# A two-layer GELU network by Winograd-Strassen products: sums written over dead blocks, w2 blocks brought in one go, the first layer's sums stored one superblock later

## The chip, the cores and the metric

One core of a Trainium2 chip runs the kernel. The metric is the device time of one execution in microseconds (us), given as the median over several executions. Its engines have their own instruction streams, each in order: TensorE (PE in the profile, with its weight loads as PEld), VectorE (DVE), ScalarE (ACT), GpSimd (POOL) and SyncE (SP). In this kernel SP and POOL issue the DMA transfers (SPq and POOLq in the profile).

## The reference

```python
def reference(x, w1, w2):          # x 8x1024x1024, w1 1024x4096, w2 4096x1024, fp32
    h = x @ w1
    h = 0.5 * h * (1 + np.tanh(np.sqrt(2 / np.pi) * (h + 0.044715 * h ** 3)))
    return (h @ w2).astype(np.float32)
```

The first two axes of x are one axis of 8192 tokens.

## The kernel before

**Strassen products.** Tokens are taken in 8 superblocks of 1024 (loop L639). In each, both matrix products are done in fp16 by seven products of half-size blocks instead of eight (tables A_TERMS for the operand from x or g, B_TERMS for that from w1 or w2, L28 to L45). Each operand is cut into 2x2 blocks named 11, 12, 21, 22. Five of the seven weight operands are a sum or difference of two blocks ("sums"; products 4, 1, 3, 7, 6), two are plain blocks (2 and 5). Likewise five x operands are differences. The weight sums are needed by every superblock, so they are made once, stored in DRAM (w1_d, w2_d) and loaded in later superblocks; the plain fp16 blocks are kept in raw_d and raw2_d.

**Memory.** Pool `up` has 26 units of 512 KB (128 partitions x 2048 fp16), shared by weight blocks, sums and x operands (all called u in the profile). Pool `tp` has 10 tiles tmp (128x512 fp32), `gcp` 4 tiles gc. There are 8 PSUM banks ps. A tile is handed out again when its last reader is done, and for a tile that is being stored this means when the DMA has landed.

**matmul1** (L277). For each of 16 chunks c of 128 columns: seven products of four matmuls (L283), in the order 4, 5, then 6 of the chunk before (`finish`, L297), 1, 2, 3, 7. Three banks take them; DVE forms the results with the `tt` helper (all its operations are recorded at L112), through tmp tiles, and ACT copies a bank (L347) and applies GELU into g (L293). Four chunks share a quad of w1 columns. In superblocks 0 and 1 a quad is a MadeQuad (L150): raw blocks, from which DVE makes five sums of 128x2048. In superblock 0 the raw blocks are loaded from w1 in fp32 and cast; in superblock 1 they come from raw_d (L160), and each sum is stored to w1_d by a POOL DMA (L192). From superblock 2 on, `load_ops` (L198) loads all seven operands of a quad. `ahead` (L305) brings the next quad step by step during the current one.

**matmul2_made** (L381) does the second product in superblocks 0 and 1: products 4, 2, 5, 1, 7, 3, 6 in this order, each of four row groups q of 16 matmuls (`product2`, L561). Where the g operand is a difference, DVE makes it into a gc tile ahead of the row group. `bring` loads w2 blocks (superblock 0: fp32 with a cast on POOL, L123; superblock 1: fp16 from raw2_d), `keep` stores the plain blocks to raw2_d, `add` makes the sums of w2, and in superblock 1 stores them to w2_d (L421). Blocks 11 and 21 come first, already during matmul1; 22 and 12 follow. Banks are evicted by ACT copies (L437, L428) and DVE additions; u and d are intermediate results that later products are added to. Outputs are stored from tmp tiles on the POOL queue (L379), at most eight POOL DMAs outstanding. In superblock 1, `split_inner` (L474) forms the parts of the sums 7 and 6 for a second level of Strassen and stores them to in_d. From superblock 2 on, `matmul2` (L599) loads w2_d and in_d and doesn't differ between the two kernels.

**x of the next superblock.** `x_cast` (L256) has POOL issue 8 DMAs that cast x to fp16 in DRAM (xb); `x_transpose` (L263) has SP issue 16 transposing DMAs into four units. Before matmul1, `XOps.make` forms five differences of x blocks on DVE.

**Order.** A list scheduler orders each engine's instructions by data and program order. `load_in_order` (L119) fixes the order of the SP DMAs that use it. `tc.issue_after` ties an instruction behind another. Each engine and each queue runs in the order so found: an instruction that waits holds all behind it on its engine.

Of the kernel before, what the change touches and what calls it, by code (L numbers as in the profile page):

```python
# [56 lines left out]
def kernel(  # L57
# [71 lines left out]
    def make_sum(ops, m, raw, rows, cols, sl=slice(None)):  # L129
# [7 lines left out]
        tt(ops[m][:, :, sl], raw[u][:, :, sl], raw[v][:, :, sl], op)  # L137

    def cast_in(dst, src, cast, staged=False):
# [10 lines left out]
    class MadeQuad:  # L150


        def __init__(self, q, first):
            self.q, self.first, self.ops = q, first, {}
            self.raw = raw_units(KH, QW)
            for m in PLAIN:
                self.ops[m] = self.raw[B_TERMS[m][0]]
            if not first:
                for b, t in self.raw.items():
                    nc.sync.dma_start(out=flat(t), in_=raw_d[q][:, BLOCKS.index(b), :])  # L160
# [28 lines left out]
        def sum(self, m, sl=slice(None)):  # L189
            make_sum(self.ops, m, self.raw, KH, QW, sl)  # L190
            if not self.first:
                nc.gpsimd.dma_start(out=w1_d[self.q][:, m - 1, :], in_=flat(self.ops[m]))  # L192
# [84 lines left out]
    def matmul1(xs, sb):  # L277
# [14 lines left out]
        def gelu(b, c, src):  # L292
            nc.scalar.activation(out=g[b][:, c, :], in_=src, func=GELU)  # L293

# [10 lines left out]
        def ahead(q, step):  # L305

            if q == NI // QC:
                return
            if sb > 1:
                if step == 0:  # L310
                    quads.append(load_ops(w1_d[q], raw_d[q], ORDER, KH, QW))
                return
            if step == 0:
                quad = MadeQuad(q, sb == 0)
                quads.append(quad)
# [6 lines left out]
        if sb == 0:  # L322
            quads.append(MadeQuad(0, True))
            xs.make(5)
# [14 lines left out]
        for c in range(NI):  # L339
            q, j = divmod(c, QC)  # L340
            if j == 0:
                ahead(q + 1, 0)
            w = (quads[q] if sb > 1 else quads[q].ops, slice(j * P, (j + 1) * P))
            pb, qb = psum(), psum()
# [36 lines left out]
    def matmul2_made(sb, g, keep_w1):  # L381
# [3 lines left out]
        sums = {}  # L385
        blocks = None

        def bring(bs, staged):
            for q in range(NI // QC):
                for b in bs:  # L390
                    t = unit(QC, OH)
                    raw[b].append(t)
                    if sb:
                        nc.sync.dma_start(out=flat(t), in_=raw2_d[q][:, BLOCKS.index(b), :])
                        continue
                    for j in range(0, QC, 2):
# [3 lines left out]
                            w2v[int(b[1]) - 1, int(b[0]) - 1, :, c:c + 2, :],  # L400
                            pool_copy,
                            staged,
# [9 lines left out]

        def add(m):
            u, op, v = B_TERMS[m]
            sums[m] = []
            for q in range(NI // QC):
                t = unit(QC, OH)
                tt(t, raw[u][q], raw[v][q], op)
# [11 lines left out]

        v, c21 = {}, {}
        pb, qb, rb = [], [], []
        bring(("11", "21"), False)
        add(4)
        for q, ps in product2(g, 4, pieces(4), pb, True, True):
            v[q] = temp()
            nc.scalar.copy(out=v[q], in_=ps)  # L437
        bring(("22",), True)
        if sb == 0:
            xb = x_cast(1, pool_last[0])  # L440
        keep(("11", "21"))
        for q, ps in product2(g, 2, pieces(2), pb, False):
            _, c21[q] = copy_out("21", q, ps)
        add(1)
        u, d = halves()[1], halves()[1]
        for q, ps in product2(g, 5, pieces(5), qb, True):
            tt(u[q], v[q], ps, SUB)
            tt(d[q], u[q], c21[q], SUB)
        add(7)
        bring(("12",), True)  # L450
        for q, ps in product2(g, 1, pieces(1), rb, True):
            tt(d[q], d[q], ps, ADD)
        if sb == 0:
# [228 lines left out]
```

## Time and profile before

| | us |
|---|---|
| median of 6 runs (1583.75 to 1588.0) | 1585.97 |
| the profiled execution | 1583.75 |
| its span in the trace | 1582.0 |
| PE busy in the span | 1549.0 (98%) |
| DVE busy | 1011.6 (64%) |
| ACT busy | 457.7 (29%) |
| POOL busy | 224.8 (14%) |

The median of the runs is 2.2 us above the profiled execution, and that execution 1.75 above its span. Mean DMA traffic is 227 GB/s over the span. The largest groups that the change touches:

```profile
## 5 line engine op out<-in xcount | busy, mean ns | idle before, releaser
...
L293 ACT ACTIVATE g<-tmp 128x512 f16<-128x512 f32 x256 | 161.1, 630 | 297.5 <-DVE tmp L112 297.4
...
L112 DVE TENSOR_TENSOR u<-u 128x2048 f16<-128x2048 f16 (+2 forms) x150 | 163.7, 1127 | 17.8 <-DMA u<-raw_d 9.0
...
L112 DVE TENSOR_TENSOR gc<-g,g 128x2048 f16<-128x2048 f16 x112 | 137.1, 1257 | 20.1 <-PE ps L566 20.1
```

A row reads: line, engine, operation, what it writes and reads with partitions x elements and type, and the count; then its busy time in us and the mean of one in ns; then the engine's idle time just before such instructions, and what ended most of it. So 20.1 us of DVE idle time before the g differences were ended by a matmul that had read the gc tile.

DMA rows give the transfers, their size and the median time from issue to landing:

```profile
u<-raw_d SPq DMA_DIRECT2D x128, 512.0 KB, 8.2
w_d<-u POOLq DMA_DIRECT2D x40, 512.0 KB, 7.1
out_dram<-tmp POOLq DMA_DIRECT2D x72, 256.0 KB, 3.1
raw_d<-u SPq DMA_DIRECT2D x32, 512.0 KB, 7.9
xb<-in_x_dram POOLq DMA_DIRECT2D x56, 256.0 KB, 11.4
```

### The profile page before, as it was taken

To read this page: it belongs to the slowest core of one execution; us is meant where nothing else is said; L and a number is where in the kernel's file an instruction comes from. 1 tells how busy PE (TensorE), PEld (TensorE's weight loads), DVE (VectorE), ACT (ScalarE), POOL (GpSimd) and SP (SyncE) were. 2 spreads that over 40 slices of the span, in tenths; PEclk is the share of its full clock that TensorE was granted. 3 is DMA by queue.
4 is the path that set the end of the run, shared out by engine and by line. 5 is a ranking of instruction groups with operands and counts; after the bars stand their busy time and mean duration, and the time that the engine had idled before them with its cause. 6 is when DMAs were issued, how large, how long until landed. Compare 5 with 4: busy or idle time off the path is not lost.

```text
span 1582.0 us, 20386 instructions
## 1 busy us (share of the span) xinstructions
PE 1549.0 (98%) x7808; PEld 766.6 (48%) x7808; DVE 1011.6 (64%) x1263; ACT 457.7 (29%) x776; POOL 224.8 (14%) x306
## 2 busy tenths in 40 slices
PE   7999989999989999999999999999999999999998
PEld 4444434444434455444554445544555445544455
DVE  7877767668755566555675557656475565755564
ACT  5641014420144211441124410344103430044200
POOL 2244321012400013000120001200012001200000
PEclk9999999999999999999999999999999999999999
DMA  9988698645984567735686346954469545663155
GB/s 318 340 322 282 173 381 279 192 180 210 387 286 133 187 239 262 253 97 200 253 283 224 119 173 253 330 182 176 151 240 363 150 171 189 239 271 133 54 213 187
DMA packets 167362, 358.93 MB, mean 227 GB/s; under 512 B 72928, under 2 KB 79072, under 8 KB 166368
## 3 DMA queue, kind: packets, MB, share of 16 engines
q1 hardware_dynamic: 148672, 285.26, 51.2%
q0 software_dynamic: 18592, 72.37, 13.9%
q8 instruction: 61, 1.00, 0.2%
q14 instruction: 37, 0.30, 0.1%
HBM read 278.92 MB, written 93.32 MB: 235 GB/s over the span
## 4 chain that ended last, share of the span: by engine, by line
PE 85%; DMA 7%; DVE 4%; issue 2%; POOL 0%; ACT 0%; SPq 0%; DVEq 0%; ACTq 0%; POOLq 0%
PE ps L283 45%; PE ps L566 35%; PE ps L522 6%; DVE u L112 3%; DMA u<-w_d 2%; DMA out_dram<-tmp 2%; DVE tmp L112 1%; DMA u<-raw_d 1%; DMA in_d<-u 1%; DMA gc<-in_w_dram 1%; DMA u<-in_d 0%; DVE gc L112 0%; DMA u<-in_x_dram 0%; POOL in_d L487 0%; ACT g L293 0%
## 5 line engine op out<-in xcount | busy, mean ns | idle before, releaser
L283 PE MATMUL ps<-u 128*128 128x512 f16 x3584 | 784.2, 381 | 19.4 <-DVE tmp L112 14.7
L112 DVE TENSOR_TENSOR tmp<-tmp,ps 128x512 f32<-128x512 f32 x548 | 375.2, 686 | 306.1 <-ACT tmp L347 119.3
L283 PEld LDWEIGHTS <-u 128*128 128x128 f16 x3584 | 351.5, 98 | 449.7 <-issue 27.8
L566 PE MATMUL ps<-u,gc 128*128 128x512 f16 x1792 | 389.4, 379 | 0.0
L566 PEld LDWEIGHTS <-gc 128*128 128x128 f16 x1792 | 175.2, 98 | 211.6
L293 ACT ACTIVATE g<-tmp 128x512 f16<-128x512 f32 x256 | 161.1, 630 | 297.5 <-DVE tmp L112 297.4
L566 PE MATMUL ps<-u,g 128*128 128x512 f16 x1024 | 224.3, 379 | 0.4 <-DVE u L112 0.2
L293 ACT ACTIVATE g<-ps 128x512 f16<-128x512 f32 x256 | 151.9, 596 | 101.8 <-PE ps L283 101.6
L112 DVE TENSOR_TENSOR u<-u 128x2048 f16<-128x2048 f16 (+2 forms) x150 | 163.7, 1127 | 17.8 <-DMA u<-raw_d 9.0
L566 PEld LDWEIGHTS <-g 128*128 128x128 f16 x1024 | 100.2, 98 | 120.6 <-issue 1.8
L112 DVE TENSOR_TENSOR gc<-g,g 128x2048 f16<-128x2048 f16 x112 | 137.1, 1257 | 20.1 <-PE ps L566 20.1
L379 POOL DMA_DIRECT2D out_dram<-tmp x72 | 39.5, 548 | 774.6 <-ACT tmp L616 632.3
L112 DVE TENSOR_TENSOR u<-u,ps 128x512 f32<-128x512 f32 x152 | 101.2, 682 | 71.6 <-ACT tmp L623 37.3
L522 PE MATMUL ps<-u,gc 128*128 128x256 f16 x960 | 109.7, 273 | 0.8
L347 ACT COPY tmp<-ps 128x512 f32<-128x512 f32 x128 | 72.9, 570 | 94.1 <-PE ps L283 94.1
L522 PEld LDWEIGHTS <-gc 128*128 128x128 f16 x960 | 93.8, 98 | 12.8 <-issue 1.6
L112 DVE TENSOR_TENSOR gc<-u 128x2048 f16<-128x2048 f16 x60 | 73.2, 1221 | 38.9 <-PE ps L566 38.9
L112 DVE TENSOR_TENSOR tmp<-ps,tmp 128x512 f32<-128x512 f32 x128 | 88.4, 690 | 10.0 <-DMA out_dram<-tmp 4.1
L112 DVE TENSOR_TENSOR u<-tmp,ps 128x512 f32<-128x512 f32 x32 | 22.0, 687 | 83.7 <-PE ps L566 74.0
L112 DVE TENSOR_TENSOR u<-g,g 128x2048 f16<-128x2048 f16 x48 | 59.6, 1280 | 0.0
L616 ACT COPY tmp<-ps 128x512 f32<-128x512 f32 x24 | 14.1, 586 | 152.0 <-PE ps L566 152.0
L545 POOL TENSOR_TENSOR u<-u,tmp 128x512 f32<-128x512 f32 x12 | 26.2, 2180 | 198.8 <-DMA u<-in_d 140.0
(33 smaller groups left out, 354.6 us busy)
## 6 DMA issues: line engine op xcount, KB each, us to landing
u<-w_d SPq DMA_DIRECT2D x192, 512.0 KB, 8.4
u<-raw_d SPq DMA_DIRECT2D x128, 512.0 KB, 8.2
u<-in_d SPq DMA_DIRECT2D x84, 512.0 KB, 7.4
gc<-in_w_dram SPq DMA_DIRECT2D x48, 512.0 KB, 5.8
w_d<-u POOLq DMA_DIRECT2D x40, 512.0 KB, 7.1
out_dram<-tmp POOLq DMA_DIRECT2D x72, 256.0 KB, 3.1
raw_d<-u SPq DMA_DIRECT2D x32, 512.0 KB, 7.9
xb<-in_x_dram POOLq DMA_DIRECT2D x56, 256.0 KB, 11.4
```

The costliest lines, as they stand in the source:

```text
L112: nc.vector.tensor_tensor(out=out, in0=in0, in1=in1, op=op)
L283: nc.tensor.matmul(bank, lhsT=ops[m][:, k, cs], rhs=xs[m][:, k, :], start=(first and k == 0), stop=(k == KH - 1), skip_group_check=not first,)
L293: nc.scalar.activation(out=g[b][:, c, :], in_=src, func=GELU)
L347: nc.scalar.copy(out=v, in_=pb)
L379: return queue.dma_start(out=out2[r0:r0 + P, o0:o0 + OH], in_=src)
L522: nc.tensor.matmul(bank[:, i * HO:(i + 1) * HO], lhsT=t[:, c, i * P:(i + 1) * P], rhs=y[j][:, c, :], start=(first and i == 0 and c == 0), ...
L545: nc.gpsimd.tensor_tensor(out=part("11"), in0=part("11"), in1=pair(u), op=ADD)
L566: nc.tensor.matmul(banks[q], lhsT=a, rhs=pieces[c // QC][:, c % QC, :], start=(first and c == 0), stop=(c == NI - 1), skip_group_check=not ...
L616: nc.scalar.copy(out=c21, in_=ps)
```

## The change

Six edits, all in superblocks 0 to 2; the matmuls and their order stay as they are.

1. Sums 7, 3 and 6 of w2 are written in place over the raw blocks 21, 22 and 11 (`over=`), which no later product reads.
2. u and d lie in tmp tiles: u is a DVE copy of product 4's bank (before, an ACT copy v, then a separate u), d overwrites the copy-out tile of block 21, and the results of products 7 and 6 are added in place and stored from there.
3. Blocks 22 and 12 are both brought right after product 4, and ScalarE casts them instead of POOL, after the last GELU of matmul1 (`late_copy`). All four raw blocks are kept at once after that.
4. x of the next superblock is cast after the second store of block 21, and transposed ahead of product 1, in both superblocks 0 and 1 (before: superblock 1's followed matmul1's program text, with the cast behind the last store of the superblock before).
5. The raw2_d loads and the transposes of superblock 1 go in program order on SP, and `split_inner` comes ahead of products 7 and 3 instead of behind products 7 and 6.
6. The w1 sums are stored in superblock 2 instead of 1. Superblock 2 therefore makes its quads from raw blocks (16 loads, 20 sums on DVE, 20 stores) instead of loading 28 operands; superblocks 3 to 7 load them as before.

```diff
-        def __init__(self, q, first):
-            self.q, self.first, self.ops = q, first, {}
+        def __init__(self, q, first, store):
+            self.q, self.store, self.ops = q, store, {}
...
         def sum(self, m, sl=slice(None)):
             make_sum(self.ops, m, self.raw, KH, QW, sl)
-            if not self.first:
+            if self.store:
                 nc.gpsimd.dma_start(out=w1_d[self.q][:, m - 1, :], in_=flat(self.ops[m]))
...
-            if sb > 1:
+            if sb > 2:
...
-                quad = MadeQuad(q, sb == 0)
+                quad = MadeQuad(q, sb == 0, sb == 2)
...
+        def late_copy(out, in_):
+            with tc.issue_after(gelu_last[0].ins):
+                nc.scalar.copy(out=out, in_=in_)
...
                     if sb:
-                        nc.sync.dma_start(out=flat(t), in_=raw2_d[q][:, BLOCKS.index(b), :])
+                        load_in_order(flat(t), raw2_d[q][:, BLOCKS.index(b), :])
...
-        def add(m):
+        def add(m, over=None):
...
-                t = unit(QC, OH)
+                t = unit(QC, OH) if over is None else raw[over][q]
...
-        v, c21 = {}, {}
+        u, d = {}, {}
         pb, qb, rb = [], [], []
-        bring(("11", "21"), False)
+        bring(("11", "21"), pool_copy, False)
         add(4)
         for q, ps in product2(g, 4, pieces(4), pb, True, True):
-            v[q] = temp()
-            nc.scalar.copy(out=v[q], in_=ps)
-        bring(("22",), True)
-        if sb == 0:
-            xb = x_cast(1, pool_last[0])
-        keep(("11", "21"))
+            u[q] = temp()
+            nc.vector.tensor_copy(out=u[q], in_=ps)
+        bring(("22",), late_copy, True)
+        bring(("12",), late_copy, True)
+        keep(("21", "22", "11", "12"))
         for q, ps in product2(g, 2, pieces(2), pb, False):
-            _, c21[q] = copy_out("21", q, ps)
+            at, d[q] = copy_out("21", q, ps)
+            if q == 1:
+                xb = x_cast(sb + 1, at)
         add(1)
-        u, d = halves()[1], halves()[1]
         for q, ps in product2(g, 5, pieces(5), qb, True):
-            tt(u[q], v[q], ps, SUB)
-            tt(d[q], u[q], c21[q], SUB)
-        add(7)
-        bring(("12",), True)
+            tt(u[q], u[q], ps, SUB)
+            tt(d[q], u[q], d[q], SUB)
+        add(7, over="21")
+        blocks = x_transpose(xb, load_in_order)
         for q, ps in product2(g, 1, pieces(1), rb, True):
             tt(d[q], d[q], ps, ADD)
-        if sb == 0:
-            blocks = x_transpose(xb, load_in_order)
-        keep(("22", "12"))
-        for q, ps in product2(g, 7, pieces(7), rb, False):
-            c = temp()
-            tt(c, u[q], ps, ADD)
-            store(sb, "11", q, c)
         if sb:
             split_inner(7, pieces(7))
-        add(3)
-        add(6)
+        for q, ps in product2(g, 7, pieces(7), rb, False):
+            tt(u[q], u[q], ps, ADD)
+            store(sb, "11", q, u[q])
+        add(3, over="22")
+        add(6, over="11")
+        if sb:
+            split_inner(6, pieces(6))
         for q, ps in product2(g, 3, pieces(3), qb, False):
             copy_out("12", q, ps)
         for q, ps in product2(g, 6, pieces(6), qb, False):
-            c = temp()
-            tt(c, d[q], ps, ADD)
-            last = store(sb, "22", q, c)
-        if sb:
-            split_inner(6, pieces(6))
+            tt(d[q], d[q], ps, ADD)
+            last = store(sb, "22", q, d[q])
         return last, blocks
...
-        if sb and sb + 1 < NSB:
-            blocks = x_transpose(x_cast(sb + 1, last), nc.sync.dma_start)
-        if sb == 0:
-            last, blocks = matmul2_made(sb, g, quad.keep_raw)
-        elif sb == 1:
-            last, _ = matmul2_made(sb, g, None)
+        if sb < 2:
+            last, blocks = matmul2_made(sb, g, None if sb else quad.keep_raw)
         else:
+            if sb + 1 < NSB:
+                blocks = x_transpose(x_cast(sb + 1, last), nc.sync.dma_start)
             last = matmul2(sb, g)
```

More of the change, by code (lines that the diff above doesn't have):

```diff
@@ L137, in make_sum @@
         tt(ops[m][:, :, sl], raw[u][:, :, sl], raw[v][:, :, sl], op)
+    gelu_last = [None]
     def cast_in(dst, src, cast, staged=False):
@@ L292, in gelu @@
         def gelu(b, c, src):
-            nc.scalar.activation(out=g[b][:, c, :], in_=src, func=GELU)
+            gelu_last[0] = nc.scalar.activation(out=g[b][:, c, :], in_=src, func=GELU)
         late = None
@@ L322, in matmul1 @@
         if sb == 0:
-            quads.append(MadeQuad(0, True))
+            quads.append(MadeQuad(0, True, False))
             xs.make(5)
@@ L342, in matmul1 @@
                 ahead(q + 1, 0)
-            w = (quads[q] if sb > 1 else quads[q].ops, slice(j * P, (j + 1) * P))
+            w = (quads[q] if sb > 2 else quads[q].ops, slice(j * P, (j + 1) * P))
             pb, qb = psum(), psum()
@@ L385, in matmul2_made, with bring @@
         sums = {}
-        blocks = None
-        def bring(bs, staged):
+        def late_copy(out, in_):
+            with tc.issue_after(gelu_last[0].ins):
+                nc.scalar.copy(out=out, in_=in_)
+        def bring(bs, cast, staged):
             for q in range(NI // QC):
@@ L400, in bring @@
                             w2v[int(b[1]) - 1, int(b[0]) - 1, :, c:c + 2, :],
-                            pool_copy,
+                            cast,
                             staged,
```

## The prediction

> **What bounds the kernel now.** I read four views: the engine totals of the page, the busy table cut at the stage ends, the waits of TensorE (PE), and the timeline around the places the first three point to. The totals show an almost full PE:
>
> ```profile
> PE 1549.0 (98%) x7808; PEld 766.6 (48%) x7808; DVE 1011.6 (64%) x1263; ACT 457.7 (29%) x776; POOL 224.8 (14%) x306
> ```
>
> The change leaves the matmuls and their order alone, so only idle PE and PE at a low clock can be won. The stage table says where these are: matmul1 and matmul2 of superblock 0, of superblock 1, then matmul1 of superblock 2, then of 3.
>
> ```profile
> core 0: us, PE busy (x) PEld busy (x) DVE busy (x) ACT busy (x) POOL busy (x), PEclk, DMA share, GB/s
> 17.30:121.10 103.80, 100.10 (x449) 44.01 (x450) 85.39 (x114) 58.47 (x94) 38.18 (x36) 0.98 0.94 327
> 121.10:218.30 97.20, 97.01 (x449) 43.63 (x446) 67.26 (x62) 8.26 (x14) 34.33 (x36) 1.00 0.82 252
> 218.30:326.20 107.90, 100.58 (x450) 44.45 (x450) 78.59 (x105) 44.83 (x78) 17.87 (x34) 0.97 0.74 253
> 326.20:423.50 97.30, 97.08 (x450) 43.84 (x448) 73.20 (x83) 8.27 (x14) 27.00 (x48) 1.00 0.68 258
> 423.50:528.40 104.90, 98.99 (x450) 44.31 (x449) 55.07 (x80) 45.53 (x79) 6.09 (x12) 0.97 0.65 218
> ...
> 622.20:718.90 96.70, 96.70 (x450) 43.83 (x448) 55.00 (x80) 45.74 (x79) 5.48 (x11) 1.00 0.62 202
> ```
>
> Each stage has 448 matmuls, and the undisturbed one takes 96.7 us (0.216 each). Against that, matmul1 of superblock 1 loses 11.2 and of superblock 2 loses 8.2; the two matmul2 between lose 0.5 and 0.6. So 20.5 us is the ceiling. The first stage (7.1 lost) isn't touched. The waits name VectorE (DVE):
>
> ```profile
> PE ps L283 <- DVE tmp L112: 14.7, 11, 5.9
> PE ps L283 <- DVE u L112: 4.3, 3, 2.5
> ```
>
> The timeline of the first gap gives the chain backwards:
>
> ```profile
> 176.44 21.26 SPq L120 DMA_TRANSPOSE u<-xb  x16
> 197.75 8.38 SPq L120 DMA_DIRECT2D raw_d<-u  x8
> 206.23 47.88 SPq L160 DMA_DIRECT2D u<-raw_d  x16
> 217.40 1.23 DVE L112 TENSOR_TENSOR u<-u 128x2048 f16<-128x2048 f16 x1 [8.72 <-DMA u<-raw_d]
> 220.04 0.68 DVE L112 TENSOR_TENSOR tmp<-u,ps 128x512 f32<-128x512 f32 x1
> 227.11 9.72 PE L283 MATMUL ps<-u 128*128 128x512 f16 x32 [4.80 <-DVE tmp L112]
> ...
> 439.84 5.50 PE L283 MATMUL ps<-u 128*128 128x512 f16 x15 [5.91 <-DVE tmp L112]
> ```
>
> SyncE (SP) issues late loads, then 21 us of transposes, then 8 stores of raw w2, and only at 206 the w1 loads for the next superblock. They land at 217. DVE sits 8.7 us on them, with the evictions of product 6 queued behind: their out stores go late, the 10 tmp tiles run short, and PE idles 4.80 and some small pieces, 7.3 in all. The clock then stands at half until 232.4, which makes up nearly all of the other 3.9. The second gap (5.91, and half clock to 444, 2.3) has the other root of this kind: stores of inner sums (in_d) and w2 sums fill the queue from 403 on, and an out store issued at 425.40 takes 13.57 us in the chain of waits, which keeps a tmp tile.
>
> **The change, part by part.** *In-place sums.* Sums 7, 3, 6 overwrite raw blocks 21, 22, 11; u and d stay in tmp tiles. 12 units of sums and 4 of u, d fall away out of 26. No DVE sum is removed. What it buys is time of loading: the last 8 w2 pieces, spread over 141–176 before, find buffers as soon as product 4 has read its operands (134.9). 16 keeps at 1.05 each (8 in 8.38 above) and the 16 transposes (21.3) follow; transposes end near 177 instead of 198, quad 0's w1 loads are issued right behind and, at the 10 us of the row 208.87 (u<-raw_d in the chain), land near 187. DVE needs them from about 191: five x sums and five w1 sums at 1.2 make 11, done near 202, and product 6's first eviction is due at 207.7. Slack some 5 us. So the 8.72 goes, and the evictions of product 6 leave on time.
>
> What is late next: w1 quad 2 takes units that product 6 reads to the last group (216.3); at 10.6 us (median of u<-raw_d at 200–260) they land at 227, and DVE meets the first of their sums after some six chunk evictions, a wait of a few us with evictions behind it. Chunk 1 has 4 free tmp tiles by then, so I take 1.2 lost (0 to 4) for matmul1 of superblock 1, against 11.2.
>
> *Copies.* u is a DVE copy of a bank, not an ACT copy: 4 per superblock by 0.69 (the row of a 128x512 bank operation), 5.5 for both. DVE is 69% busy there (67.26 of 97.20), PE waits for none: 0. Without cover 2.8 each.
>
> *ScalarE casts.* 16 casts at 1041 ns (row L145) are 16.6 us on ACT, which is 8% busy in that stage, in place of 24.6 on POOL (row L123, 1558 each). Product 5 needs block 22 at 148.7; the eighth cast can end near 144 (loads land in 5.5). Hidden, 5 us of cover. The last casts end near 155, ahead of their keeps.
>
> *A new wait.* Here is a cost. In the new DVE order, d += product 1 of row groups 0 and 1 stand ahead of the difference of g that product 1's row group 2 multiplies. The second d waits for row group 1's last matmul, so PE idles through 0.69 + 1.22 and two hand-overs, about 2.3 us. Whether the clock falls is the question, and trace rows on both sides are near:
>
> ```profile
> 17.30 1.78 PE L283 MATMUL ps<-u 128*128 128x512 f16 x4 [2.45 <-DVE u L112]
> 18.00:19.00 1.00, 1.00 (x3) 0.15 (x1) 0.38 (x1) 0.00 (x0) 1.00 (x2) 0.50 1.21 292
> 24.36 5.91 PE L283 MATMUL ps<-u 128*128 128x512 f16 x26 [1.46 <-DVE u L112]
> ```
>
> After 2.45 idle, PE ran at half clock (0.50) from 17.5 to 20.6, a loss of 1.6; after 1.46 it kept full clock. 2.3 is nearer to 2.45: I take 2.3 + 1.5 = 3.8 (2.0 to 3.9), so matmul2 of superblock 0 becomes 101.0.
>
> The Trainium skill, page "TensorE: Matmul & The Clock Gate", Part 1, says the clock falls after at least one idle window of about 3.4 us; by that rule 2.3 us would cost no clock, and the total would be 1.5 lower. The startup row contradicts it, and the measurement goes into the sum.
>
> *Moved x work.* The 8 xb casts of a superblock go behind the second 21 store. Stores 3 and 4 of block 21 queue behind them on POOL, and the d differences of groups 2 and 3, which overwrite the stored tiles, wait for their landings. Before, at the same place, the casts were issued at 144.3 to 147.7 and landed in 4.1 (median), and the two stores behind them, issued at 148.70 and 149.95, took 9.7 and 9.0: landed at 159. Those two d (0.6 each), four in-place sums (1.16 each in a row of four, 4.6) and the first d += (0.7) stand ahead of the second d +=, which can start at 169.4: they must start by 169.4 - 0.7 - 4.6 - 1.2 = 162.9. Covered by 4 us. For superblock 2, xb and transposes leave matmul1 of superblock 1 (226–298) for the middle of its matmul2: DMA moves, no PE work.
>
> *Superblock 1, matmul2.* in_d and w2 sums leave earlier (split 7 ahead of product 7, split 6 ahead of product 3), so fewer stand ahead of the out stores at 403–430. Some DVE sums now wait for in_d landings (8.3 to 9.7 us) with evictions behind: I take 0.3 (0 to 2) on 97.3: 97.6.
>
> *w1 sums.* 20 stores of 0.5 MB (10.5 MB) leave superblock 1, and superblock 2 makes the sums itself: 20 at 1.27 = 25.4 more on DVE (55.1 to 80.5 of 97, fits), 12 loads fewer, 20 stores more. In its first 23 us, 10 sum stores, 4 quad loads and out stores are 5.2 + 2.1 + 2.1 = 9.4 MB, 410 GB/s. The row of 200–260 shows what this traffic does: 402 to 415 GB/s at a share of 1.0, with out stores landing in 9. Quad 2's loads then come about 3 us late. I take 3.5 lost (0.5 to the full 8.2) against 8.2.
>
> **Sum.** Four stages after: 101.0 + 97.9 + 97.6 + 100.2 = 396.7. Before: 97.2 + 107.9 + 97.3 + 104.9 = 407.3. Saved 10.6. The profiled execution took 1583.75 (span 1582.0 and 1.75 around it), so 1573.15; the median of the runs is 2.2 above that execution, so as a median 1575.4.
>
> **Rivals.** *The second gap stays* (0.22). For it: 9.4 MB in 23 us is saturation, the very state in which the first gap stood. Superblock 2 keeps its 8.2, the saving falls by 4.7: 1580.1. Against it: no in_d stores pile up there any more.
>
> *It does not bring the loads forward* (0.08). The transposes wait for xb, which waits for a full queue, or the late loads wait longer for their buffers, so quad 0 is late by more than its 5 us. At 8 to 10 late, superblock 1 keeps 8 to 10 of its 11.2 us; superblock 2 wins 4.7, and 4.1 are lost in the two matmul2: 1.8 to 3.8 saved, 1582.2 to 1584.2, counted as no change.
>
> *Slower: a d that waits for its store* (0.10). The wait just named, of d of group 3 for the 21 store behind the xb casts. With the longest rows (xb 13.8, then an out store's 13.57, from 143.4) the landing is at 170.7, 7.8 late: PE idles 7.8 + 2.3, and the half clock costs 2.3 more (as after 5.91), 12.4 in all. Against it stand the 10.0 won in superblock 1 less 0.3; where superblock 2 keeps its 8.2 nothing else does, and the time is 1588.7. Break-even is a landing at 168, and from 171.2 on it is slower by over 0.2%; 3 us beyond the longest rows, 1592. Against it: the rows of the same place land at 159. For it: 16 keeps of 0.5 MB (8.4 MB) now run in these microseconds, where before the DMA share fell to 0.46 by 160–170.
>
> **Numbers.** Forecast 0.60, second gap 0.22, not forward 0.08, slower mechanism 0.10. 0.2% is 3.2 us, about what a measurement of this kernel can tell from no change. Faster by more than that: all of the forecast and second-gap cases, 0.82. Same: the third case and 0.02 of the last, 0.10. Slower: 0.08. Range: below, 1.2 + 0.3 + 3.5 + 1.8 of my losses not occurring give 1568.6, so 1568; above, the second gap kept and the upper bounds in superblock 1's two stages (2.8 + 1.7) give 1584.6, so 1584.
>
> **What would show it.** Right: no wait of DVE for raw_d loads ahead of product 6's evictions, transposes of superblock 1 ending near 177, stages of 101.0, 97.9, 97.6, 100.2, one PE wait of about 2.3 on DVE's gc in product 1 followed by a clock of 0.50. Wrong: an out store's landing over 9 us ahead of matmul1 of superblock 2 with idle PE (second gap), xb issued after 150 (third), a DVE wait on an out store or raw2 keep before 175 (fourth).

## The result and the profile after

| | us |
|---|---|
| before, median of 38 runs (1583.75 to 1589.46) | 1586.85 |
| changed kernel, median of 17 runs (1579.76 to 1591.78) | 1582.93 |
| ratio, 95% interval | 0.998 (0.9972 to 0.9988) |
| profiled execution of the changed kernel (span 1576.7) | 1578.52 |

The change saves 3.9 us, 0.2%. Measured twice more, with 7 and 5 runs of it, it saved 6.9 and 5.3 us (ratios 0.9961 and 0.9963). The forecast was 10.6. So the sign was right and the size was not, and the runs spread over 12 us where those of before spread over 6.

The busy table of the changed kernel, cut at its stage ends (same order and columns as before):

```profile
122.50:223.60 101.10, 98.50 (x449) 44.10 (x448) 75.19 (x77) 21.14 (x26) 12.21 (x23) 0.98 0.87 274
223.60:321.20 97.60, 97.23 (x450) 43.84 (x449) 69.32 (x95) 45.05 (x78) 3.08 (x6) 1.00 0.36 126
321.20:418.30 97.10, 96.82 (x449) 43.82 (x448) 82.90 (x94) 5.91 (x10) 34.88 (x64) 1.00 1.01 334
418.30:519.80 101.50, 98.59 (x449) 44.17 (x448) 66.24 (x92) 45.23 (x78) 11.85 (x23) 0.98 0.64 209
```

The forecast for these four was 101.0, 97.9, 97.6 and 100.2. In this execution they sum to 397.3 against 396.7. That closeness is luck: two more traces, below, give 399.9 and 401.1. Of the 11.2 us that superblock 1's matmul1 lost, all but 0.9 are gone, as forecast. At the eviction of product 6, where VectorE came late before because it sat 8.72 us on a load, it now waits for TensorE:

```profile
213.46 0.69 DVE L112 TENSOR_TENSOR tmp<-tmp,ps 128x512 f32<-128x512 f32 x1 [4.16 <-PE ps L567]
```

TensorE's waits have changed places:

```profile
PE ps L285 <- ACT tmp L349: 3.9, 3, 2.9
PE ps L567 <- DVE gc L112: 2.6, 1, 2.6
```

The wait on gc is the new one in product 1; the 2.9 on ACT's tmp is the start of superblock 2, at 430.02. There VectorE sits on a w1 load, with evictions behind it:

```profile
419.03 7.28 DMA u<-raw_d
426.41 1.23 DVE L112 TENSOR_TENSOR u<-u 128x2048 f16<-128x2048 f16 x1 [4.29 <-DMA u<-raw_d]
430.02 10.34 PE L285 MATMUL ps<-u 128*128 128x512 f16 x40 [2.90 <-ACT tmp L349]
```

The first row is from the chain that ended last; in it, the load leaves right behind a sum of VectorE that ended at 419.02. The timeline shows the wait in product 1, and the queue of SP around it, with the clock just behind:

```profile
137.41 29.14 SPq L120 DMA_DIRECT2D raw_d<-u  x16
167.49 25.21 SPq L120 DMA_TRANSPOSE u<-xb  x16
192.82 57.79 SPq L162 DMA_DIRECT2D u<-raw_d  x16
166.56 4.63 DVE L112 TENSOR_TENSOR u<-u 128x2048 f16<-128x2048 f16 x4
171.10 1.28 DVE L112 TENSOR_TENSOR tmp<-tmp,ps 128x512 f32<-128x512 f32 x2
172.29 4.63 DVE L112 TENSOR_TENSOR gc<-g,g 128x2048 f16<-128x2048 f16 x4
173.57 22.58 PE L567 MATMUL ps<-u,gc 128*128 128x512 f16 x96 [2.60 <-DVE gc L112]
174.00:175.00 1.00, 1.00 (x4) 0.29 (x2) 1.00 (x2) 0.00 (x0) 0.00 (x0) 0.50 2.17 311
```

The in-place sum 7 (166.56, four pieces), both additions to d (171.10), and only then the g difference that row group 2 needs (172.29): PE idles 2.60 us and then runs at half clock (0.50 in each of the three us from 174 to 177).

But this execution took 1578.52 and the median run 1582.93. A trace of one execution could not say where the other runs lose their time, and the four stages are not the whole: this execution is 5.2 us under the profiled one of before, while the stages alone are 10.0 better. Of the 4.8 between, 1.4 lie ahead of these stages (the first matmul1 takes 102.8 to 106.1 us over the traces of all kernels), 0.4 behind the fourth stage, and 3.0 at the end of the span, where nothing computes:

```profile
1568.00:1573.00 5.00, 1.07 (x10) 0.70 (x8) 0.80 (x2) 0.00 (x0) 0.00 (x0) 1.00 0.57 211
1573.00:1576.70 3.70, 0.00 (x0) 0.00 (x0) 0.00 (x0) 0.00 (x0) 0.00 (x0) 0.53 0.00 0
```

The same two rows of before:

```profile
1576.00:1581.00 5.00, 1.30 (x12) 0.92 (x10) 1.04 (x2) 0.00 (x0) 0.00 (x0) 0.98 0.56 210
1581.00:1582.00 1.00, 0.00 (x0) 0.00 (x0) 0.00 (x0) 0.00 (x0) 0.00 (x0) 0.50 0.00 0
```

In both kernels the last stores end some 3 us after the last matmul (DMA 0.57 and 0.56 of 5 us). Then the changed kernel's span goes on for at least 3.7 us with no engine and no DMA at work, that of before for 1 to 2.

### The profile page after: what moved, and what is told of

Same layout as the page of the kernel before. It is cut to its first block, busy times and chain, and to the rows that moved or that the text cites. A ratio compares the mean times of both kernels' runs of the same rounds, so it can differ in the third digit from the quotient of the medians.

```text
span 1576.7 us, 20360 instructions
## 1 busy us (share of the span) xinstructions
PE 1548.7 (98%) x7808; PEld 768.0 (49%) x7808; DVE 1029.2 (65%) x1291; ACT 467.9 (30%) x784; POOL 200.3 (13%) x290
## 4 chain that ended last, share of the span: by engine, by line
PE 87%; DMA 8%; DVE 3%; issue 1%; ACT 1%; SPq 0%; POOL 0%; DVEq 0%; ACTq 0%
PE ps L285 47%; PE ps L567 35%; PE ps L523 6%; DMA u<-w_d 2%; DMA raw_d<-u 2%; DMA gc<-in_w_dram 2%; DMA u<-raw_d 1%; DVE u L112 1%; DVE tmp L112 1%; DVE gc L112 1%; DMA u<-in_d 0%; DMA u<-in_x_dram 0%; SPq L120 0%; ACT u L147 0%; ACT g L295 0%
## 5 line engine op out<-in xcount | busy, mean ns | idle before, releaser
L112 DVE TENSOR_TENSOR tmp<-tmp,ps 128x512 f32<-128x512 f32 x580 | 396.4, 686 | 302.8 <-ACT tmp L349 113.7
L112 DVE TENSOR_TENSOR u<-u 128x2048 f16<-128x2048 f16 (+2 forms) x170 | 183.4, 1112 | 18.5 <-DMA u<-raw_d 11.4
L295 ACT ACTIVATE g<-ps 128x512 f16<-128x512 f32 x256 | 151.9, 596 | 98.3 <-PE ps L285 97.9
L567 PEld LDWEIGHTS <-g 128*128 128x128 f16 x1024 | 100.2, 98 | 119.5
L112 DVE TENSOR_TENSOR gc<-g,g 128x2048 f16<-128x2048 f16 x112 | 133.0, 1222 | 15.8 <-PE ps L567 15.8
L112 DVE TENSOR_TENSOR u<-u,ps 128x512 f32<-128x512 f32 x144 | 95.8, 682 | 69.4 <-ACT tmp L624 38.1
L349 ACT COPY tmp<-ps 128x512 f32<-128x512 f32 x128 | 73.0, 570 | 95.7 <-PE ps L285 95.7
L112 DVE TENSOR_TENSOR u<-tmp,ps 128x512 f32<-128x512 f32 x24 | 16.5, 688 | 74.7 <-PE ps L567 65.0
L617 ACT COPY tmp<-ps 128x512 f32<-128x512 f32 x24 | 14.1, 586 | 152.0 <-PE ps L567 152.0
L624 ACT COPY tmp<-ps 128x512 f32<-128x512 f32 x24 | 14.0, 585 | 134.3 <-PE ps L567 132.1
```

The lines of the kernel that those rows point to most:

```text
L112: nc.vector.tensor_tensor(out=out, in0=in0, in1=in1, op=op)
L295: gelu_last[0] = nc.scalar.activation(out=g[b][:, c, :], in_=src, func=GELU)
L349: nc.scalar.copy(out=v, in_=pb)
L567: nc.tensor.matmul(banks[q], lhsT=a, rhs=pieces[c // QC][:, c % QC, :], start=(first and c == 0), stop=(c == NI - 1), skip_group_check=not ...
L617: nc.scalar.copy(out=c21, in_=ps)
L624: nc.scalar.copy(out=c12, in_=ps)
```

## The experiments

Theory A: VectorE waits that vary from run to run. Theory B: the ends of the execution. In the tables, the stages are matmul2 of superblock 0, matmul1 and matmul2 of superblock 1, matmul1 of superblock 2; "end" is from the last matmul to the end of the span. Each row is one trace.

| kernel | stages | end |
|---|---|---|
| before | 97.3, 107.8, 97.3, 104.9 | 4.7 |
| before again | 97.3, 108.5, 98.1, 105.4 | 4.6 |
| changed | 101.2, 97.6, 97.1, 101.5 | 7.6 |
| changed again | 102.6, 97.3, 97.1, 102.9 | 7.7 |
| changed, third | 103.2, 98.0, 97.1, 102.8 | 7.7 |
| early differences | 96.7, 96.9, 97.9, 101.2 | 7.7 |
| sums stored in superblock 1 | 101.2, 102.2, 98.5, 96.7 | 4.7 |
| late stores on GpSimd | 103.5, 97.8, 99.3, 118.7 | 7.7 |
| the same with early differences | 96.7, 96.9, 97.1, 103.3 | 7.7 |
| casts last | 101.0, 98.4, 105.8, 102.2 | 7.7 |
| x put back | 101.6, 97.6, 96.7, 105.6 | 7.7 |
| x put back, early differences | 96.7, 97.0, 96.7, 106.3 | 7.6 |
| early differences, 8 memsets on GpSimd | 96.7, 96.9, 97.7, 100.9 | 7.6 |
| early differences, 24 loads on SP | 96.7, 96.9, 97.1, 101.9 | 7.6 |
| early differences, 64 memsets on VectorE | 96.7, 96.9, 98.4, 102.3 | 7.7 |
| all at once | 97.0, 97.0, 96.7, 105.4 | 7.6 |
| ScalarE stores, early differences | 96.7, 96.9, 97.5, 111.8 | 6.9 |
| ScalarE stores, x put back, early differences | 96.7, 97.0, 96.7, 109.4 | 6.8 |
| early differences, sums in superblock 1 | 96.7, 98.1, 98.7, 97.3 | 4.7 |
| the same again | 96.7, 97.3, 98.7, 96.7 | 4.6 |

**The two kernels again.** Nothing edited.

> The changed kernel once more, unchanged, for a second trace. Its four stages came out in the first trace within 0.6 us of the forecast sum (397.3 against 396.7), yet the median of its runs (1582.9) is 4.4 us above that profiled execution. Theory A (waits that vary): in another execution a VectorE instruction waits longer for a DMA landing, in matmul2 of superblock 0 or at the start of matmul1 of superblock 1 or 2; then a trace with a time over 1581 shows more than 2.6 and 2.9 us of idle TensorE there, and TensorE's last matmul ends later than 1569. Theory B (the ends): the time between the last landing and the end of the span, in which nothing is recorded (4.5 us in the first trace, 1.6 in that of before), or the startup makes the difference, and TensorE needs the same time from the first matmul to the last, within 1 us.

> The kernel before once more, for a second trace. Theory A: its last matmul ends near 1577.3 again, within 1 us, and its idle places are the same two (4.8 and 5.9 us). Theory B: the same in this, and its unrecorded end is nearer to 4.5 us than to 1.6, which would lift the time to 1586 to 1587, the median of before.

Changed: 1580.28 (7 runs, 1577.07 to 1584.52); before: 1586.66 (8 runs), against 1587.20 for all the runs of before on this chip. The traced run of the changed kernel took 1580.28, just under the 1581 that theory A names, and shows what the theory says: VectorE waited for the stores of block 21 ahead of the d differences, and the idle time of PE grew by nearly as much.

```profile
165.11 0.69 DVE L112 TENSOR_TENSOR tmp<-tmp 128x512 f32<-128x512 f32 x1 [0.77 <-DMA out_dram<-tmp]
166.39 0.69 DVE L112 TENSOR_TENSOR tmp<-tmp 128x512 f32<-128x512 f32 x1 [0.59 <-DMA out_dram<-tmp]
174.01 22.58 PE L567 MATMUL ps<-u,gc 128*128 128x512 f16 x96 [4.05 <-DVE gc L112]
```

0.77 + 0.59 = 1.36 of waiting, and 4.05 against 2.60 of idle time, 1.45 more. The start of superblock 2 lost more too: 5.59 us of waiting for the w1 load and 3.89 us of idle PE, against 4.29 and 2.90. What was expected of before did not come: its traced run took 1588.40, its last matmul ended at 1581.96 and not within 1 us of 1577.3. The two idle places are nearly the same (4.51 and 6.05 us); of the 4.6 more, 0.7 lie ahead of the first matmul1, 1.8 in it and 2.0 in the four stages. So the time ahead of the end varies in both kernels. Theory B, as I put it for single runs, fails: the end is 4.6 to 4.7 in both traces of before and 7.6 to 7.7 in both of the changed kernel. It is not the chance of one run; the changed kernel has it each time. "1.6 against 4.5" in the expectation is the same 3 us, counted from the last landing.

**Early differences.** The four g differences of product 1 are made ahead of sum 7.

```diff
+        made = [diff(g, 1, q) for q in range(NQ)]
         add(7, over="21")
         blocks = x_transpose(xb, load_in_order)
-        for q, ps in product2(g, 1, pieces(1), rb, True):
+        for q, ps in product2(g, 1, pieces(1), rb, True, made=made):
...
```

`diff` makes one g difference into a gc tile, as `product2` did; `product2` takes the ones already made.

> The four g differences of product 1 are made ahead of the in-place sum 7 and of the additions to d, so that product 1's row group 2 waits for no eviction. If the new wait costs what the trace shows (2.6 us idle and 3 us at half clock, 1.6), the time falls by 4.2 us against the changed kernel, to about 1578.7 as a median, and the spread over 1584 goes too if it was this wait that varies with the landing of block 21's keep. Rival: VectorE is continuously busy from 157 to 178, so what is pushed back (sum 7, the differences of product 7) is late for product 7 instead: 1582 to 1583, with a wait of TensorE on a sum or a gc tile between products 1 and 7.

1573.31 (4 runs, 1572.64 to 1574.28), ratio 0.9912 (0.9897 to 0.9926): 7.0 us under the changed kernel on the same chip, more than the 4.2 expected. Superblock 0's matmul2 is at 96.7, with no clock loss, and no product in it waits. The wait costs 4.5 to 6.5 us (101.2, 102.6, 103.2 in the changed kernel's three traces against 96.7), not 3.8. A little of the rival shows in superblock 1: product 7 waits 0.57 us for a g difference, and the stage takes 97.9 instead of 97.1.

**Sums stored in superblock 1.** The last edit undone alone.

```diff
-            if sb > 2:
+            if sb > 1:
...
-                quad = MadeQuad(q, sb == 0, sb == 2)
+                quad = MadeQuad(q, sb == 0, sb == 1)
...
```

> The w1 sums are stored in superblock 1 again and superblock 2 loads its 28 operands; all other edits stay. Theory (the stores saturate the DMA engines wherever a matmul1 starts beside out stores): superblock 1 loses 3 to 8 us, superblock 2 only about 1 of its 4.8, time 1582 to 1587. Rival (superblock 1 starts with its transposes and two quads loaded, so it has room for 10 stores; what the stores met in superblock 2 is the tail of the stores of inner sums): superblock 1 stays at 97.6 to 99, superblock 2 near 97, time 1578 to 1580.

1578.06 (11 runs, 1574.71 to 1589.09), ratio 0.9947 (0.9931 to 0.9962), 2.2 us under the changed kernel on this chip. The stage times took the theory's side: superblock 1's matmul1 takes 4.9 us more (102.2), superblock 2's is at 96.7. Moving the stores moved the loss from one start to the other. The time is the rival's (1578 to 1580), because the end of the span is 4.7 again, which neither side had foreseen: the 3 us at the end belong to this edit.

**Late stores, and both.** The stores of quads 0 and 1 are written at the end of their quads, tied behind a GELU.

```diff
-            if self.store:
+            if self.store and self.q > 1:
...
+        def store_late(self):
+            with tc.issue_after(gelu_last[0].ins):
+                for m in SUMS:
+                    nc.gpsimd.dma_start(out=w1_d[self.q][:, m - 1, :], in_=flat(self.ops[m]))
...
+            if sb == 2 and q < 2 and j == QC - 1:
+                quads[q].store_late()
```

> The changed kernel, but in superblock 2 the w1 sums of quads 0 and 1 are stored at the end of their own quad's chunks instead of as soon as they are made; nothing else differs. Theory (the ten early stores beside quad loads and out stores saturate the DMA engines, a quad's load lands late, VectorE waits for it with evictions behind, as at 426.41 in the first trace): the stage of superblock 2 falls from 101.5 to 102.9 to about 97.5, as in superblock 1, which makes quads without stores; time 4 to 5 us under the changed kernel, about 1577. Rival (the load is late because its units are free late, whatever the traffic): stage still over 100.5, time within 1 us of the changed kernel.

> Early g differences of product 1 and late stores together. If the two causes are independent: 1573.3 less 4 to 5, about 1569. If the idle time only moves to another place, above 1572.

1583.46 (12 runs, 1578.37 to 1600.77) and 1575.41 (12 runs, 1570.89 to 1591.57), where the theory had about 1577 and 1569: nothing gained. They didn't do what they should: in the second trace GpSimd issued these ten stores from 397.8 to 414.5, as early as the sums were made. They test nothing about the stores. But the first one's trace is of its slowest run, and shows where that run lost:

```profile
360.49 48.00 SPq L120 DMA_TRANSPOSE u<-xb  x16
420.57 11.44 DVE L112 TENSOR_TENSOR u<-u 128x2048 f16<-128x2048 f16 x10 [18.32 <-DMA u<-raw_d]
```

The transposes for superblock 2 took 48 us on SP, with all of that superblock's w1 loads queued behind them, and VectorE sat 18 us on the first load. PE then idled 4.57, 8.87 and 2.16 us.

**Casts last.** The xb casts behind the fourth store of block 21.

```diff
-            if q == 1:
+            if q == NQ - 1:
                 xb = x_cast(sb + 1, at)
```

> The changed kernel, with the eight xb casts behind the fourth store of block 21 instead of the second, so that no 21 store queues behind them. Theory (the time varies from 1577 to 1592 because the d of row groups 2 and 3 waits for 21 stores that queue behind the casts, ahead of product 1's third g difference): no VectorE wait on an out store, the idle time ahead of row group 2 is 2.6 or less, the runs lie within 4 us of each other and their median near 1578. Rival (the spread has another place): the same spread of some 10 us and a median over 1580.

1587.48 (11 runs, 1583.73 to 1592.62). VectorE no longer waited for an out store, the idle time was 2.52 and the stage 101.0: that part held, and this is what the order alone costs, 2.5 us of idle time and 1.8 of clock. The median did not fall, since superblock 1 has the same code. Its transposes came later, VectorE waited 7.87 us for a store of inner sums, and PE 6.17:

```profile
379.58 1.29 DVE L112 TENSOR_TENSOR u<-u 128x1024 f16<-128x1024 f16 x2 [7.87 <-DMA in_d<-u]
382.06 16.14 PE L567 MATMUL ps<-u,gc 128*128 128x512 f16 x64 [6.17 <-DVE gc L112]
```

**x of superblock 2 put back**, alone and with early differences (theory C).

```diff
-            if q == 1:
+            if q == 1 and sb == 0:
                 xb = x_cast(sb + 1, at)
...
-        blocks = x_transpose(xb, load_in_order)
+        if sb == 0:
+            blocks = x_transpose(xb, load_in_order)
...
+        if sb and sb + 1 < NSB:
+            blocks = x_transpose(x_cast(sb + 1, last), nc.sync.dma_start)
```

> The changed kernel, with only the x of superblock 2 put back: cast behind the last store of superblock 0 and transposed beside superblock 1's matmul1, as before the change. Theory C (the run-to-run spread of the changed kernel, and the late loads of superblock 2, come from the 16 transposes that now stand in superblock 1's matmul2 beside the stores of inner sums: 31 us in good runs, 48 in the one of 1600.8, against 22 before, with the quad loads of superblock 2 queued behind them on SP): the transposes take 22 to 25 us, the stage of superblock 2 falls from 101.5 to 102.9 to under 99, no run is over 1586, median 1576 to 1579. Rival (the traffic beside matmul1 of superblock 1 has no room, or superblock 2 is late for the units alone): superblock 1 or 2 as slow as in the changed kernel, median over 1580.

> The same with the early g differences of product 1. If theory C and the wait in product 1 are the two causes: both gone, runs within 5 us of each other, median 1568 to 1570, 4 to 5 under the kernel with early differences alone (1573.3). If the transposes were not the cause: 1573 again with single runs over 1580.

1583.95 (12 runs, 1580.35 to 1587.65) and 1578.63 (5 runs, 1578.15 to 1579.5), both over what was expected. Part of theory C stands: the transposes take 21.6 us again, superblock 1's matmul2 is at its best (96.7), and the spread of the second kernel is 1.4 us. The rest fell: the first still spreads over 7.3 us, with two runs over 1586, and superblock 2's matmul1 takes longer (105.6 and 106.3 against 101 to 103), though its loads are issued from 382 and 376 on, where the changed kernel's began at 391.7. In the first, VectorE waits 7.36 us for a w1 load again; in the second for a store of a w1 sum, whose unit the next sum is to overwrite:

```profile
421.43 1.23 DVE L112 TENSOR_TENSOR u<-u 128x2048 f16<-128x2048 f16 x1 [7.41 <-DMA w_d<-u]
423.31 17.04 PE L285 MATMUL ps<-u 128*128 128x512 f16 x68 [6.56 <-DVE tmp L112]
```

**The ten stores on ScalarE**, behind the second chunk of their quad, where the order of ScalarE's instructions holds them back; with early differences, and in the second kernel with x put back too. The edit is shown against the late stores.

```diff
-                    nc.gpsimd.dma_start(out=w1_d[self.q][:, m - 1, :], in_=flat(self.ops[m]))
+                    nc.scalar.dma_start(out=w1_d[self.q][:, m - 1, :], in_=flat(self.ops[m]))
...
-            if sb == 2 and q < 2 and j == QC - 1:
+            if sb == 2 and q < 2 and j == 1:
```

> Early g differences, and the w1 sums of quads 0 and 1 stored in superblock 2 by ScalarE, whose instruction order puts the stores behind the second chunk of each quad; the trace of the kernel with late stores showed that GpSimd issued them early all the same, so it tested nothing. Theory (ten early stores make a quad's load or a freed unit late, VectorE waits with evictions behind): the stage of superblock 2 falls from about 101 to 97 to 98, median 4 us under 1573.3. Rival (the late unit is freed by something else, the transposes or the in_d stores): stage still over 100.

> The same with x of superblock 2 put back. There the stage of superblock 2 took 106.3 with 6.6 us idle, and VectorE waited 7.4 us for a w1 store that held a unit. Theory: stage 97 to 98.5, median 1569 to 1571 (1578.6 less 8), and no run more than 3 us from it. Rival: stage over 103, median 1576 or more.

1582.28 and 1580.32 (5 runs each), where about 1569 to 1571 was expected: superblock 2 is worse, 111.8 and 109.4. The first waits got shorter (2.08 us of idle PE at 419.04 in the second, against 6.56), but at 434.31 VectorE waited 4.93 us and at 434.46 ScalarE 4.42 us, both for these stores, and PE lost 3.29 there and more behind it. In the first, VectorE waited 8.68 us for such a store at 438.57, and PE 7.11. Delaying a store delays the unit that it holds: the waits came later and were longer, and the expected gain was wrong.

**The end of the span.** Three attempts to find it, all on the kernel with early differences: eight memsets on GpSimd, 24 loads of 64 bytes on SP, 64 memsets on VectorE.

```diff
+    pad = consts.tile([P, 1], F32, name="pad")
+    for _ in range(8):
+        nc.gpsimd.memset(pad, 0.0)
```

> The kernel with early g differences, and eight one-column memsets on GpSimd at the start, which change nothing else. From the last matmul to the end of the span it is 7.6 to 7.7 us in all three traces where superblock 2 makes its sums, with an 8 KB instruction transfer among the last rows, and 4.6 to 4.7 in the three others, without one. Theory (a block of GpSimd's instructions begins just at the end of the program, and its fetch holds the last wait): with other block positions the end takes 4.7 again and the time falls by 3 to about 1570.3. Rival (the end depends on something in the work itself, such as the stores of the last superblock): 7.7 and 1573.3 again.

> The kernel with early g differences and 24 loads of 64 bytes on SP after matmul1 of superblock 3, whose data nobody reads. Eight more instructions on GpSimd left the end of the span at 7.6 us. SP has 24 instructions fewer than in the kernel before. Theory (SP's last block of instructions is fetched only at the end): the end takes 4.7 us again, and the time falls by 3 to 1570.3. Rival (not a fetch, or not SP's): 7.7 us and 1573.3.

> Early g differences and 64 one-column memsets on VectorE at the start. The end of the span stayed at 7.6 us with 8 more instructions on GpSimd and with 24 more on SP, although those moved SP's last code fetch away from the end. Theory (it is VectorE's code position): 4.7 us at the end. Rival: 7.6 again, and the cause stays open.

1573.33 (12 runs, two of them over 1583), 1581.97 (12 runs) and 1575.44 (5 runs, one of them over 1583). The ends: 7.6, 7.6, 7.7; the stages are like those of early differences alone, within 1.1 us. The 24 loads were meant for the place behind superblock 3's matmul1, but were issued at the start of the program, among the first loads of x and ahead of those of w1, so the first matmul1 began at 24.96 instead of 18: most of their 8 us is this. But they did take the last instruction transfer out of the last 9 us of the span, and the end stayed at 7.6. So it is not that transfer. What it is stays open.

**All at once**, before the causes were clear: x put back, early differences, and the 24 loads.

> Early g differences, x of superblock 2 put back, and the 24 loads on SP. If the three effects add: 1565 to 1567, faster than both kernels. If the end does not move, 1568 to 1570.

1585.97 (11 runs), far over the 1565 to 1570 expected: the loads at the start (first matmul1 at 24.96) and superblock 2 at 105.4 eat the rest.

**Early differences and sums stored in superblock 1**, and once more beside the changed kernel. Both edits were shown above.

> Early g differences, w1 sums stored in superblock 1 as before. If the costs add: the end takes 4.7 us (3 less), superblock 1 loses 4 to 5 at its start, superblock 2 is at 96.7, so 1570 to 1573. If the early differences push other work back onto superblock 1's start, over 1575.

> The changed kernel a third time, beside the fastest one on the same chip. From the two earlier sessions: median 1580 to 1583, runs spread over 7 us or more; in the trace the wait ahead of product 1's row group 2 between 2.6 and 4.1 us, the stage of superblock 2 between 101 and 103, the end of the span 7.6.

> Early g differences and w1 sums stored in superblock 1, again. If the two causes found (the wait in product 1, the sums of superblock 2 with the 3 us at the end) make up the difference: median 1571 to 1573, 8 to 10 us under the changed kernel on the same chip, end of the span 4.7, stages of superblocks 1 and 2 within 2 us of 96.7 each. If the first trace of it was a lucky one: over 1575.

1572.19 (4 runs), ratio 0.9904 (0.9890 to 0.9917); again on another chip 1567.08 (4 runs, 1564.94 to 1567.99), ratio 0.9873 (0.9859 to 0.9886), with the changed kernel at 1581.44 (5 runs, 0.9963) beside it. This version beats both kernels; by how much differs between the two measurements (15.9 and 19.7 us under before), and the second lies under the 1571 to 1573 expected. The changed kernel's third trace kept to what was expected of it, a wait of 3.46 us in product 1 among it, but its five runs spread over 4.0 us and not 7 or more. The first and last of its four stages in the second trace:

```profile
122.50:219.20 96.70, 96.70 (x449) 43.83 (x448) 73.12 (x76) 21.14 (x26) 16.01 (x30) 1.00 0.96 314
...
415.20:511.90 96.70, 96.70 (x449) 43.83 (x448) 55.05 (x80) 45.69 (x78) 5.03 (x10) 1.00 0.57 175
```

Both are at the undisturbed 96.70, with PE busy throughout. Against the changed kernel's third trace: 6.5 in superblock 0, 0.7 and 6.1 in the two matmul1, 3.1 at the end, less 1.6 in superblock 1's matmul2, 14.8 together; the medians differ by 14.4. So the two causes, the order in product 1 and the sums made and stored in superblock 2, make up the difference between this version and the changed kernel. Making the sums and storing them were moved together, so these runs don't say which of the two costs. With the stores in superblock 1 its matmul1 took 102.2 in the one trace without early differences and 98.1 and 97.3 in the two with them: VectorE waited 5.18 us for a w1 load there, against 2.16 and 1.63. Why that load came later is not tried.

## Why the prediction was right and wrong

- **The bound and the first gap: right.** Ceiling, chain and cure were as put: superblock 1's matmul1 falls from 107.8 and 108.5 to 97.3 to 98.0, where 97.9 was forecast. On the way one number was off: 16 keeps took 29.1 us (1.8 each, not 1.05), so the transposes ended at 192.7 and not near 177. The chain had more slack than the 5 us given: 16 us later, VectorE still waited 4.16 us for TensorE at product 6's first eviction (213.46).
- **Copies, ScalarE casts, earlier w2 and inner sums: right.** The copies show as a PE wait of 0.3 us, the others as none; superblock 1's matmul2 took 97.1 in all three traces (97.6 forecast).
- **The new wait: right mechanism, too small.** The order alone costs what was forecast: casts last, where no store is late, has 2.52 us idle and a stage of 101.0. The step that failed is "landed at 159", with its "covered by 4 us". In the changed kernel's three traces the last two stores of block 21 were issued at 153.4 to 156.3, not at 148.7 and 150.0, took 11.0 to 11.3 us and landed at 164.5 and 165.8, 165.0 and 166.3, 166.1 and 167.6. The casts ahead of them had been taken as landing in 4.1; that is the median of before's casts and transposes together, the casts alone had 6.4, and in the first trace they took 8.0 to 13.8. So there was no cover: in the second and third trace the last d difference began only at 166.4 and 167.7, and PE idled 4.05 and 3.46 us. The stage took 101.2, 102.6 and 103.2, a mean of 1.3 over the forecast. Beside the idle time, 1.9, 1.9 and 3.1 us of it are lost to half clock, which lasted twice as long in the third. It is the slower rival in its mild form, and its sign came: a VectorE wait on an out store before 175.
- **The half clock behind that wait: right in the sum, on weak ground.** "2.3 is nearer to 2.45" takes the length of the idle stretch as what decides. The clock did fall in all seven traces that have the wait (2.52 to 4.36 us), but elsewhere it fell after 2.08 us and stayed after 3.57 (last section).
- **The w1 sums in superblock 2: too small, and moved to the wrong place.** "I take 3.5 lost" was 4.8, 6.2 and 6.1. The wait is the forecast one, a w1 load that comes late (4.29, 5.59 and 5.17 us of VectorE), beside traffic of 400 GB/s and more; its size was wrong. The step priced the late load by bandwidth alone. In the chain of the first trace two loads stand behind each other: one lands after 11.68 us, sums follow, and the next load leaves only behind the last of them and takes 7.28. Where x was put back or the stores were delayed, some waits name stores that hold a unit, and they come later instead of going. Storing in superblock 1 cost little in its place: with early differences its matmul1 takes 0.4 to 1.2 us more and its matmul2 0.8.
- **What no step contained:** 3.0 us at the end of the span in every kernel whose superblock 2 makes its sums and stores them on GpSimd (2.2 with ten of the stores on ScalarE). The sum took the 1.75 outside the span and everything behind the fourth stage as unchanged. This is the largest single miss, and its cause stays open.

Means of the traces: the four stages 408.3 before (two) and 399.5 after (three), 8.8 saved; less 3.0 at the end, 5.8. The three comparisons of medians say 3.9, 6.9 and 5.3. So the forecast's 10.6 lost 3.0 to the end, 2.2 to superblock 2 and 1.3 to product 1, and the other 1.7 lay on the better side. The rest of the spread isn't settled: the run at 1600.8 lost it to 48 us of transposes in superblock 1's matmul2. With x put back and early differences, five runs lay within 1.4 us; with early differences and x as in the change there were runs over 1583 in two measurements of three, those with the memsets. That speaks for the transposes, but the numbers of runs are small, and late transposes alone are not enough: in the first trace of early differences with the sums in superblock 1 they took 41.8 us, and superblock 2's matmul1 still took 97.3.

## What to carry to other kernels

When a wait is removed, read the built order of the engine that releases the next one: here a g difference behind four sums and two additions cost more than any of the forecast terms but the main one, and making it ahead of them took all of it back. A store is not over when it is issued; price the buffer that it holds until it lands, at the place where that buffer is wanted next. And take more than one trace before pricing a wait with little cover, because the median pays for the landings that one trace doesn't show.

## What the runs showed of the hardware

- TensorE's clock fell to 0.50 after only 2.60 us of idle time (the row at 174.00), and once after 2.08 (ScalarE stores, x put back). In the kernel with early differences it stayed at 1.00 after 3.57. So in these traces the length of one idle stretch doesn't settle it. The Trainium skill, page "TensorE: Matmul & The Clock Gate", Part 1, puts the fall behind at least one idle window of about 3.4 us; the falls after 2.60 and 2.08 come earlier. The row behind the 2.08, then the wait of 3.57 and the row behind it:

```profile
419.04 17.39 PE L290 MATMUL ps<-u 128*128 128x512 f16 x72 [2.08 <-DVE tmp L112]
421.00:422.00 1.00, 1.00 (x4) 0.29 (x2) 0.09 (x1) 0.00 (x0) 1.00 (x3) 0.50 1.43 352
...
426.82 26.43 PE L285 MATMUL ps<-u 128*128 128x512 f16 x120 [3.57 <-ACT tmp L349]
427.00:428.00 1.00, 1.00 (x6) 0.48 (x5) 1.00 (x2) 0.00 (x0) 0.20 (x1) 1.00 1.04 422
```

- The half clock behind the wait in product 1 lasted 3.4 us in the changed kernel's first two traces and 6.8 in the third.
- SP needed 21.3 to 22.3 us for the sixteen transposes of one superblock's x where the DMA engines moved 90 to 204 GB/s in that time, 24.6 to 25.6 right behind the sixteen keeps (216 GB/s in the changed kernel), and 30.3 to 48.0 beside stores of w2 and inner sums (328 GB/s in the changed kernel, 265 in the slowest).
- From the last matmul to the end of the span: 4.6 to 4.7 us, 7.6 to 7.7, or 6.8 to 6.9 with ten stores on ScalarE. It is the same to 0.1 us for the three kernels with more than one trace, and the last four stores are of the same size in all.
